# A hybrid decoder block on one Trainium2 core: memory attention one head ahead, x turned once, differential heads left unscaled, last plain panels loaded sooner

## The chip, the cores and the metric
The kernel runs on one core of one Trainium2 chip. The metric is the device time of one execution in microseconds (us). The kernel before was timed in three runs: median 1875.49, from 1874.84 to 1875.73. A core has five engines with an instruction queue each: PE (matrix products and transposes; PEld is its weight load), DVE (VectorE), ACT (ScalarE), POOL (GpSimd) and SP, which only issues transfers here.

## The reference, cut to what matters
x is 1024 tokens by 1024 float32 channels, mem 256 tokens. All weights are float32.

```python
def _hybrid_mixer(h, w_in, ...):          # h = rmsnorm(x) * g_mix
    qa, ka, va, qb, kb, vb, fl, ga, gb = jnp.split(h @ w_in, IN_OFFSETS, axis=-1)
    ...
        a1 = softmax(causal(qa1 @ ka1 * scale + rel)); a2 = softmax(causal(qa2 @ ka2 * scale + rel))
        oa = (a1 - lam * a2) @ va          # 4 differential heads, 128 wide
        ob = softmax(causal(qb @ kb * scale + (c_q - c_k))) @ vb   # 8 forgetting heads
    ya = _rmsnorm(oa, g_subln) * (1.0 - lambda_init)
    return (sigmoid(ga) * (ya @ w_diff_out) + sigmoid(gb) * (yb @ w_fox_out)) @ w_o
def _memory_cross_attention(h, mem_n, w_q, w_kv, w_o):   # 4 heads, 256 wide, 256 keys
    return (softmax(q @ k * 1/16) @ v) @ w_o
def reference(x, mem, ...):
    x = x + _hybrid_mixer(_rmsnorm(x, g_mix), ...)
    x = x + _memory_cross_attention(_rmsnorm(x, g_mem_q), _rmsnorm(mem, g_mem_kv), ...)
    x = x + relu(_rmsnorm(x, g_mlp) @ w1) ** 2 @ w2
    return _rmsnorm(x, g_final)
```

## The kernel before, in words
Activations lie transposed, channels on the partitions, in two halves of 512 tokens. Each float32 operand is kept as a high part, rounded by an ACT copy, and a low part, what is left (a subtraction on DVE or POOL). `mm3` (L100 to L102) makes a product of three matmuls: high by high, low by high, high by low. `wload` (L89 to L96) brings a weight panel into one of two `raw` buffers by an SP transfer and splits it: ACT L95 the high part, POOL (or DVE) L96 the low part. The code is written as stages; a scheduler orders each engine's instructions among them by what it models, so the order on an engine isn't that of the code. Every queue runs in order.

- **Front.** For each of 8 blocks of 128 tokens, `norm1_block` loads x, squares and sums it on ACT (L144), makes 1/rms by `rstd_of` (L135 to L140: small DVE instructions and one ACT square root), scales on DVE by 1/rms and a broadcast copy of g_mix (L146), turns the result by 8 PE transposes (L165), and splits it (L168 ACT, L169 DVE) into `hT`. `xT_block` turns x itself by 8 more transposes (L178), copies it (L180) and stores it for the residual. `v_unit(0)` makes the first values from hT (tiles `vps`, 24 matmuls a block). After that `rel_tables` makes the bias rows (stored and read back through DRAM), and `p_unit(0)` the queries and keys of head 0 (tiles `pq`, `pk`, 96 matmuls).
- **Differential heads** (`scores`, `soft_block`, `pv`, units 0 to 3). Scores plus bias are reduced to their minimum (L380), ACT takes exponentials with their sum (L384), a reciprocal gives z (L385). The second branch's z is multiplied by -lambda (L431), the first branch's row by its z (L432), and L433 adds the second times its factor. PE turns the row (L456), L460 and L461 split it, L483 multiplies it with the values. Work of later stages is drawn from a list of `fillers` in between. The output's rms norm comes in `prep_a_stats`.
- **Memory attention.** For n = 0..7 (4 heads, two token halves): `m_q` makes the queries (`qp`, 48 matmuls), `m_a` goes over 4 token blocks: scores (`msc`, 6 matmuls of 256 columns into a PSUM bank of its own), minimum (L859), exponential (L860), reciprocal (L861), scaling (L862), two transposes (`mtp`, L864); then a split (`mat`, L616 and L617), the product with the values (`mop`) and its split (`mo`). `m_o` multiplies with the output weights (`mop2`, 48 matmuls) and adds to x (L885). `norm_T`, `norm_0a` and `norm_0b` run beside `m_o`; `spread` (L634 to L644, tile `sp`) lays a row of 1/rms over all partitions by PE.
- **Up, first part.** `plain_up(i, c)` multiplies one panel of w1 with one token half. The pairs (2,1) and (3,1) come after `up_weights(0)` has issued its loads and 7 weight splits (`Ring.put`, L1065 ACT and L1066 POOL) for the products that follow (`mm_u`, `o_u`, `sc_u`).

```python
        for mt in range(2):
            T.transpose(tps[mt][:, ss], e[:, mt * P : (mt + 1) * P], ident)
...
w_next, steps = up_weights(0)
do_steps(steps, 7)
for i in range(NP - 6, NP - 4):
    plain_up(i, 1)
```

Of the kernel before, what the change touches and what calls it, by code (L numbers as in the profile page):

```python
# [16 lines left out]
P = 128  # L17
# [23 lines left out]
def trunk(ctx: ExitStack, tc: tile.TileContext, a: dict, out: bass.AP):  # L41
# [40 lines left out]
    def wload(parts, name, eng=G):  # L82

        raw = wp.tile([P, WT], F32, tag="raw", name=f"raw_{name}", bufs=2)
        hl = wp.tile([P, 2 * WT], F32R, tag="hl", name=f"hl_{name}", bufs=3)
        o, views = 0, []
        off = (0, 1024)
        for src, r0, nk, c0, n in parts:
            SP.dma_start(  # L89
                raw[:, o : o + nk * n].rearrange("p (k c) -> p k c", k=nk),  # L90
                src[r0 : r0 + nk * P, c0 : c0 + n].rearrange("(k p) c -> p k c", p=P),
            )
            views.append(tuple(hl[:, x + o : x + o + nk * n].rearrange("p (k c) -> p k c", k=nk) for x in off))
            o += nk * n
        A.copy(hl[:, :o], raw[:, :o])  # L95
        eng.tensor_sub(hl[:, 1024 : 1024 + o], raw[:, :o], f32(hl[:, :o]))  # L96
        return views
# [50 lines left out]
    gmix = att.tile([P, D], F32, tag="bias", name="gmix", bufs=2)  # L148
    xf = a["x"].rearrange("b s d -> (b s) d")

    def norm1_block(sb):
        c, o = sb // 4, (sb % 4) * P
        xb = att.tile([P, D], F32, tag="e1", name=f"xb{sb}", bufs=4)
        SP.dma_start(xb, xf[sb * P : (sb + 1) * P, :])
        if sb == 0:
            SP.dma_start(ident, a["ident"])
            SP.dma_start(gmix, a["g_mix"].partition_broadcast(P))
        xn = att.tile([P, D], F32, tag="kd", name=f"xn{sb}", bufs=4)
        ss = att.tile([P, 4], F32, tag="st", name=f"ss{sb}", bufs=16)
        norm_rows(xb, xn, ss, gmix)  # L160
        for g in range(2):
            ps = bank("tp", f"n1p{sb}_{g}")
            for j in range(4):
                k = 4 * g + j
                T.transpose(ps[:, j * P : (j + 1) * P], xn[:, k * P : (k + 1) * P], ident)  # L165
            p3 = ps.rearrange("p (k s) -> p k s", k=4)
            hi, lo = (hT[c].t[i][g][:, :, o : o + P] for i in (0, 1))
            A.copy(hi, p3)  # L168
            V.tensor_sub(lo, p3, f32(hi))  # L169
        return xb  # L170

    def xT_block(sb, xb):
        c, o = sb // 4, (sb % 4) * P
        for g in range(2):
            ps = bank("o", f"xtp{sb}_{g}")
# [16 lines left out]
    def v_unit(u):  # L192
# [59 lines left out]
    def p_unit(i):  # L252
# [3 lines left out]
        w = {}  # L256
# [75 lines left out]
    def forget_prep():  # L332
# [14 lines left out]
        V.scalar_tensor_tensor(l, z, 0.0, l, ALU.min, ALU.subtract)  # L347
        lt = att.tile([8, S], F32, tag="AT", name="lt", bufs=AT_BUFS)
# [19 lines left out]
    def soft_block(i, x, qb, e, bias_of, tag):  # L368
# [1033 lines left out]
```

## Time and profile before
| | |
|---|---|
| median of three runs | 1875.49 us |
| the profiled execution's own time | 1877.76 us |
| its span | 1875.9 us |
| mean granted clock of PE | 0.988 of full speed |
| busy: PE / PEld / DVE / ACT / POOL | 1805.5 / 1505.1 / 1167.1 / 878.8 / 591.3 us |
| share of the span | 96% / 80% / 62% / 47% / 32% |
| DMA | 207.38 MB, mean 111 GB/s |

The page gives one execution: for each engine its busy time, the span in 40 slices, the chain of work that ended last, and groups of instructions by line and shape with what they waited for. The own time is what the host's timer gives for that execution; the span runs from its first to its last instruction. PE's matmuls overlap in the records, so a matmul's duration there is longer than its step to the next one. [...]

### The profile page before, as it was taken

What the parts mean: (1) busy time and instruction counts of PE and PEld (TensorE: products, weight loads), DVE (VectorE), ACT (ScalarE), POOL (GpSimd) and SP (SyncE); (2) the same over time, 40 slices, a digit from 0 to 9 for tenths busy, and PEclk for the clock granted to TensorE, in tenths of its full rate; (3) what the DMA queues carried; (4) which work ended last, traced back from release to release, by engine and by line L of the source; (5) the groups of instructions that cost most, each with busy time, mean ns of one, the idle gap of its engine ahead of it and who ended that gap; (6) DMA issues with size and microseconds to landing.
All of it is one profiled execution on the core that took longest, in us unless ns stands there. A gap on an engine that the chain in (4) does not pass through costs nothing. (4 is left out here: it accounts for less than half of the span.)

```text
span 1875.9 us, 24763 instructions
## 1 busy us (share of the span) xinstructions
PE 1805.5 (96%) x9110; PEld 1505.1 (80%) x9110; DVE 1167.1 (62%) x2209; ACT 878.8 (47%) x1628; POOL 591.3 (32%) x337
## 2 busy tenths in 40 slices
PE   7999999999999999999999998998999999999998
PEld 7779887787787778888887776787888888887786
DVE  6476877878862442223644658583777775888732
ACT  5455546766775463333443344363333345634421
POOL 2211111111223555433453423205465513132600
PEclk9999999999998999999999999999999999999999
DMA  7411111111224333354332221243444474754311
GB/s 235 140 43 43 46 55 44 54 43 53 56 67 145 105 110 101 90 191 135 112 115 66 79 101 57 88 142 96 141 146 162 136 266 149 238 180 155 123 68 45
DMA packets 234465, 207.38 MB, mean 111 GB/s; under 512 B 12603, under 2 KB 191035, under 8 KB 233832
## 3 DMA queue, kind: packets, MB, share of 16 engines
q1 hardware_dynamic: 219224, 188.76, 32.3%
q10 hardware_dynamic: 15120, 17.04, 2.7%
q8 instruction: 71, 1.16, 0.3%
q14 instruction: 50, 0.41, 0.1%
HBM read 162.73 MB, written 45.40 MB: 111 GB/s over the span
## 5 line engine op out<-in xcount | busy, mean ns | idle before, releaser
L483 PE MATMUL o<-at,v 128*128 128x256 f32 x560 | 106.8, 300 | 3.7 <-ACT at L460 2.1
L483 PEld LDWEIGHTS o<-at,v 128*128 128x128 f32 x560 | 85.2, 193 | 21.7 <-ACT at L460 11.4
L1066 POOL TENSOR_TENSOR hlu<-raw_u,hlu 128x512 fp32r<-128x512 f32 x43 | 67.8, 1590 | 108.0 <-DVE x L967 64.7
L1066 POOL TENSOR_TENSOR hls<-raw_d,hls 128x512 fp32r<-128x512 f32 x32 | 47.2, 1484 | 169.7 <-ACT hls L1065 129.4
L460 ACT CAST at<-tp 128x512 fp32r<-128x512 f32 x120 | 69.1, 585 | 43.1 <-PE tp L456 41.9
L461 DVE TENSOR_TENSOR at<-tp,at 128x512 fp32r<-128x512 f32 x120 | 81.5, 685 | 12.1 <-ACT at L460 11.3
L456 PE MATMUL tp<-ident,e 128*128 128x128 f32 x432 | 77.6, 279 | 9.4 <-DVE at L461 2.5
L1066 POOL TENSOR_TENSOR hls<-raw_u,hls 128x512 fp32r<-128x512 f32 x41 | 63.8, 1565 | 61.3 <-ACT hls L1065 50.3
L456 PEld LDWEIGHTS tp<-ident,e 128*128 128x128 f32 x432 | 52.8, 142 | 25.9 <-DVE tp L458 4.7
L96 POOL TENSOR_TENSOR hl_k<-raw_k,hl_k 128x1024 fp32r<-128x1024 f32 x8 | 19.8, 2480 | 164.8 <-ACT hl_k L95 106.9
L1065 ACT CAST hls<-raw_d 128x512 fp32r<-128x512 f32 x62 | 38.0, 620 | 69.4 <-DVE raw_d L1115 29.9
L96 POOL TENSOR_TENSOR hl_wom<-raw_wom,hl_wom 128x1024 fp32r<-128x1024 f32 x16 | 38.3, 2393 | 93.8 <-ACT hl_wom L95 93.8
L96 POOL TENSOR_TENSOR hl_gb<-raw_gb,hl_gb 128x1024 fp32r<-128x1024 f32 x16 | 38.4, 2398 | 86.6 <-ACT hl_gb L95 47.8
L289 POOL CAST kd<-kd 64x512 fp32r<-64x512 f32 x32 | 20.6, 642 | 117.4 <-ACT kd L287 79.1
L100 PE MATMUL vps<-hl_v,hT 128*128 128x256 f32 x192 | 56.6, 295 | 0.4 <-ACT hT L168 0.2
L102 PE MATMUL vps<-hl_v,hT 128*128 128x256 f32 x192 | 55.3, 288 | 1.3 <-DVE hT L169 1.3
L885 DVE TENSOR_TENSOR x<-x,mop 128x512 f32<-128x512 f32 x64 | 43.6, 683 | 20.7 <-PE mop L102 20.2
L96 POOL TENSOR_TENSOR hl_ga<-raw_ga,hl_ga 128x1024 fp32r<-128x1024 f32 x16 | 38.4, 2398 | 55.6 <-ACT hl_ga L95 43.4
L1065 ACT CAST hlu<-raw_u 128x512 fp32r<-128x512 f32 x43 | 26.3, 620 | 62.1 <-PE mm_u L1036 19.4
L101 PE MATMUL vps<-hl_v,hT 128*128 128x256 f32 x192 | 55.0, 286 | 0.0
L96 POOL TENSOR_TENSOR hl_wo<-raw_wo,hl_wo 128x1024 fp32r<-128x1024 f32 x16 | 38.8, 2427 | 50.8 <-ACT hl_wo L95 47.8
L1065 ACT CAST hls<-raw_u 128x512 fp32r<-128x512 f32 x41 | 25.1, 620 | 61.1 <-PE mm_u L1036 26.3
(813 smaller groups left out, 6436.9 us busy)
## 6 DMA issues: line engine op xcount, KB each, us to landing
raw_u<-in_w_dram SPq DMA_DIRECT2D x48, 256.0 KB, 4.2
sD<-tt SPq DMA_DIRECT2D x12, 1024.0 KB, 5.2
raw_d<-in_w_dram ACTq DMA_DIRECT2D x24, 512.0 KB, 3.4
hs<-sD SPq DMA_DIRECT2D x36, 256.0 KB, 3.9
raw_ga<-in_w_in_dram SPq DMA_DIRECT2D x16, 512.0 KB, 3.8
raw_gb<-in_w_in_dram SPq DMA_DIRECT2D x16, 512.0 KB, 3.9
raw_wo<-in_w_o_dram SPq DMA_DIRECT2D x16, 512.0 KB, 4.0
raw_wq<-in_w_q_mem_dram SPq DMA_DIRECT2D x16, 512.0 KB, 3.7
```

The source lines that it names most:

```text
L96: eng.tensor_sub(hl[:, 1024 : 1024 + o], raw[:, :o], f32(hl[:, :o]))
L100: T.matmul(ps, lh, rh, start=start, stop=False)
L101: T.matmul(ps, lh, rl, start=False, stop=False)
L102: T.matmul(ps, ll, rh, start=False, stop=stop)
L289: G.tensor_copy(t["kd"][x][r2, cs], f32(t["kd"][x][r, cs]))
L456: T.transpose(dst, Aq[qi][:, kb * P : (kb + 1) * P], ident)
L460: A.copy(at[:, 0, :], tp)
L461: V.tensor_sub(at[:, 1, :], tp, f32(at[:, 0, :]))
L483: T.matmul(o[:, :256], vv, aa, start=kp == 0 and n == 0, stop=kp == m and n == len(jobs) - 1)
L885: V.tensor_add(x2(c, j), x2(c, j), ps)
L1065: A.copy(w[0], src)
L1066: eng.tensor_sub(w[1], src, f32(w[0]))
```

## The change
It touches five places.

1. **x turned once.** `x_turn` transposes x itself (tile `xtp`), keeps the copy `xt` (one store a block, `x_store`), and computes 1/rms as before. `norm1_block` spreads 1/rms over the partitions by one transpose (`n1p`), multiplies each of the 8 channel blocks by g_mix (a per-partition column `gx_c`) and by that spread row on DVE (L204), and splits on ACT (L207) and POOL (L208). The loop is skewed: loading, turning, normalising and the first values run one or two blocks apart, and the first query panel's loads, split and part of its matmuls are drawn into the loop.
2. **Differential heads unscaled.** L432 goes; the second branch's factor becomes z2 * -lambda * s1 in one instruction (L460), with s1 the first branch's sum, kept in `dsum`. `prep_a_stats` scales EPS by s1 squared.
3. **`forget_prep`** is drawn in three pieces, with part of the next head's projections between them.
4. **Memory attention.** `m_a` becomes `m_s` (scores and softmax, two token blocks in one bank with one minimum and one reciprocal), `m_t` (transposes and split) and `m_v`; `m_s(n + 1)` is issued between `m_t(n)` and `m_v(n)`. `spread` is parted in two.
5. **Last plain panels.** Panel (2,1) is loaded with (1,1)'s, and (3,1)'s load is written ahead of both products.

```diff
+    def wload2(parts, name, eng=G):
...
+        def split():
...
+        return split
...
-    def norm1_block(sb):
...
+    def x_turn(sb):
...
+        for g in range(2):
+            ps = bank(("tp", "o")[g], f"xtp{sb}_{g}")
             for j in range(4):
                 k = 4 * g + j
                 T.transpose(ps[:, j * P : (j + 1) * P], xb[:, k * P : (k + 1) * P], ident)
...
+        A.activation(tt.rearrange("p k s -> p (k s)"), xb, AF.Square, accum_out=ss[:, 3:4])
+        A.copy(xt[:, 0:4, :], pss[0])
+        (V.tensor_copy if sb % 2 else A.copy)(xt[:, 4:8, :], pss[1])
+        rcol[sb] = (rstd_of(ss, ss[:, 3:4], D, 1), tt)
...
+    def norm1_block(sb):
...
+        ps = bank("sc", f"n1p{sb}")[:, 0:P]
+        T.transpose(ps, r.broadcast_to([P, P]), ident)
+        for g in range(2):
+            for k in range(4 * g, 4 * g + 4):
+                V.scalar_tensor_tensor(tt[:, k, :], xts[sb][:, k, :], gx_c[:, k : k + 1], ps, ALU.mult, ALU.mult)
+            hi, lo = (hT[c].t[i][g][:, :, o : o + P] for i in (0, 1))
+            t = tt[:, 4 * g : 4 * g + 4, :]
+            A.copy(hi, t)
+            G.tensor_sub(lo, t, f32(hi))
...
-                z1 = soft_block(u, 0, qb, e, bf, f"{u}a{qb}")
+                s1 = soft_block(u, 0, qb, e, bf, f"{u}a{qb}", dsum[:, qb // 4, u, qb % 4 : qb % 4 + 1])
                 fill()
                 z2 = soft_block(u, 1, qb, e2, bf, f"{u}b{qb}")
-                V.tensor_scalar(z2, z2, nlam, None, ALU.mult)
-                V.tensor_scalar(e[:, :L], e[:, :L], z1, None, ALU.mult)
+                V.scalar_tensor_tensor(z2, z2, nlam, s1, ALU.mult, ALU.mult)
                 V.scalar_tensor_tensor(e[:, :L], e2[:, :L], z2, e[:, :L], ALU.mult, ALU.add)
...
+    for sb in range(10):
+        if sb < 8:
+            x_turn(sb)
...
+        if 1 <= sb < 9:
+            norm1_block(sb - 1)
+            x_store(sb - 1)
+        if sb >= 2:
+            for _ in va0(sb - 2):
+                if sb >= 6:
+                    next(pu0[0], None)
...
-    def m_a(n):
...
+    def m_s(n):
...
+            st = small(f"mst{n}{pr}")
+            e = me[n, pr] = t2k(f"me{n}{pr}").rearrange("p (b m) -> p b m", b=2)
+            V.tensor_reduce(st[:, 0:2], ps, axis=AX.X, op=ALU.min)
...
+            V.reciprocal(st[:, 4:6], st[:, 2:4])
+            for b in range(2):
+                V.tensor_scalar(e[:, b, :], e[:, b, :], st[:, 4 + b : 5 + b], None, ALU.mult)
+
+    def m_t(n):
...
     for n in range(8):
-        m_a(n)
+        m_t(n)
+        if n < 7:
+            m_s(n + 1)
+        m_v(n)
...
-    for i in range(NP - 6, NP - 4):
-        plain_up(i, 1)
+    w31 = panel(3, 1)
+    plain_up(2, 1, w=wn)
+    plain_up(3, 1, w=w31)
```

DVE's queue in the front, where block 2 is normalised. In a name the first digits are the token block: ss2 holds its sum and 1/rms, xn2 the scaled block, vps0 the first values of block 0. Before:

```order
L146 SCALAR_TENSOR_TENSOR xn1_186<-xb1_184,ss1_187,gmix_96 128x1024
L135 TENSOR_SCALAR ss2_242<-ss2_242 128x1
L137 RECIPROCAL ss2_242<-ss2_242 128x1
L138 TENSOR_TENSOR ss2_242<-ss2_242 128x1
L139 SCALAR_TENSOR_TENSOR ss2_242<-ss2_242 128x1
L140 SCALAR_TENSOR_TENSOR ss2_242<-ss2_242 128x1
L237 TENSOR_TENSOR v0_153<-vps0_0_155,v0_153 128x128
L146 SCALAR_TENSOR_TENSOR xn2_241<-xb2_239,ss2_242,gmix_96 128x1024
L237 TENSOR_TENSOR v1_154<-vps0_0_155,v1_154 128x128
L169 TENSOR_TENSOR hT0_2_87<-n1p1_0_196,hT0_0_85 128x4x128
L169 TENSOR_TENSOR hT0_3_88<-n1p1_1_203,hT0_1_86 128x4x128
```

Now:

```order
L204 SCALAR_TENSOR_TENSOR xn2_197<-xt2_196,gx_c_77,n1p2_297 128x128 x3
L261 TENSOR_TENSOR v0_240<-vps0_0_242,v0_240 128x128
L156 RECIPROCAL ss3_273<-ss3_273 128x1
L204 SCALAR_TENSOR_TENSOR xn2_197<-xt2_196,gx_c_77,n1p2_297 128x128
L189 COPY xt3_271<-xtp3_1_279 128x512
L261 TENSOR_TENSOR v1_241<-vps0_0_242,v1_241 128x128
L157 TENSOR_TENSOR ss3_273<-ss3_273 128x1
L204 SCALAR_TENSOR_TENSOR xn2_197<-xt2_196,gx_c_77,n1p2_297 128x128
L158 SCALAR_TENSOR_TENSOR ss3_273<-ss3_273 128x1
L204 SCALAR_TENSOR_TENSOR xn2_197<-xt2_196,gx_c_77,n1p2_297 128x128
L159 SCALAR_TENSOR_TENSOR ss3_273<-ss3_273 128x1
L204 SCALAR_TENSOR_TENSOR xn2_197<-xt2_196,gx_c_77,n1p2_297 128x128 x2
```

The one 1024-wide L146 of a block and the two low-part subtractions L169 are gone from DVE. Eight 128-wide L204 stand there, and the small instructions of block 3's 1/rms (L156 to L159) stand between those of block 2. POOL's queue, which held nothing in the front but the weight panels' subtractions, now holds two L208 for each block among them.

PE's queue in memory attention, head n = 0, around its transposes (mtp00 is head 0, key half 0; me02 is head 0, token block 2, and in the change me01 is token blocks 2 and 3; mop00 is the product with the values). Before:

```order
L100 MATMUL qp20_9270<-h2_0_1_7904,hl_wq20_9266 128x512
L864 MATMUL mtp00_9179<-ident_69,me02_9219 128x128
L864 MATMUL mtp01_9180<-ident_69,me02_9219 128x128
L101 MATMUL qp20_9270<-h2_0_3_7906,hl_wq20_9266 128x512
L102 MATMUL qp20_9270<-h2_0_1_7904,hl_wq20_9266 128x512
L864 MATMUL mtp00_9179<-ident_69,me03_9234 128x128
L864 MATMUL mtp01_9180<-ident_69,me03_9234 128x128
L100 MATMUL qp20_9270<-h2_0_1_7904,hl_wq20_9266 128x512
L101 MATMUL qp20_9270<-h2_0_3_7906,hl_wq20_9266 128x512
L102 MATMUL qp20_9270<-h2_0_1_7904,hl_wq20_9266 128x512
L100 MATMUL mop00_9246<-mat0_9178,vm0_7909 128x512
L100 MATMUL mop01_9255<-mat0_9178,vm0_7909 128x512
```

Now:

```order
L116 MATMUL msc10_9150<-km_0_7822,qm1_9028 128x256
L933 MATMUL mtp00_9136<-ident_69,me01_9128 128x128
L933 MATMUL mtp01_9143<-ident_69,me01_9128 128x128
L933 MATMUL mtp00_9136<-ident_69,me01_9128 128x128
L933 MATMUL mtp01_9143<-ident_69,me01_9128 128x128
L117 MATMUL msc10_9150<-km_1_7823,qm1_9028 128x256
...
L116 MATMUL msc11_9171<-km_0_7822,qm1_9028 128x256
L117 MATMUL msc11_9171<-km_1_7823,qm1_9028 128x256
L118 MATMUL msc11_9171<-km_0_7822,qm1_9028 128x256
L116 MATMUL mop00_9193<-mat0_9135,vm0_7824 128x512
L117 MATMUL mop00_9193<-mat0_9135,vm0_7824 128x512
```

Before, two transposes stand behind each block's softmax, and the last of them a few query matmuls ahead of mop00. Now the transposes stand together among the scores of head 1, and 17 of the 24 score matmuls of head 1 lie between the last transpose and mop00.

SP's queue at the last plain panels (w1p21 is panel 2 for token half 1; u00 and u01 are the first two loads of the products that follow). Before:

```order
L89 DMA raw_w1p11_11463<-in_w1_dram 128x8x128
L1091 DMA raw_u00_11530<-in_w1_dram 128x4x128 x2
L1091 DMA raw_u01_11533<-in_w1_dram 128x4x128 x2
L89 DMA raw_w1p21_11555<-in_w1_dram 128x8x128
L89 DMA raw_w1p31_11589<-in_w1_dram 128x8x128
```

Now:

```order
L92 DMA raw_w1p11_11298<-in_w1_dram 128x8x128
L92 DMA raw_w1p21_11332<-in_w1_dram 128x8x128
L1167 DMA raw_u00_11370<-in_w1_dram 128x4x128 x2
L1167 DMA raw_u01_11373<-in_w1_dram 128x4x128 x2
L92 DMA raw_w1p31_11394<-in_w1_dram 128x8x128
```

The load of w1p21 now stands ahead of u00 and u01; that of w1p31 stays behind them.

## Rows read from the trace of the kernel before

**Rows 1.** Stretches: start:end, length, PE, PEld, DVE, ACT, POOL busy (count), clock, DMA share, GB/s.
```profile
0.00:57.00 57.00, 46.70 (x327) 41.34 (x328) 36.31 (x100) 32.85 (x72) 11.83 (x12) 1.00 0.72 211
79.00:330.00 251.00, 240.61 (x1447) 208.34 (x1446) 192.74 (x539) 135.89 (x292) 44.86 (x32) 0.99 0.16 45
1000.00:1205.00 205.00, 189.09 (x910) 152.83 (x909) 130.36 (x224) 81.83 (x156) 68.01 (x30) 0.98 0.25 79
1275.00:1300.00 25.00, 20.11 (x76) 15.71 (x75) 7.52 (x8) 7.41 (x12) 11.55 (x8) 0.86 0.39 116
```

**Rows 2.** What PE waited for, whole span: us in total, times, longest.
```profile
PE up L100 <- ACT hl_w1p L95: 4.9, 2, 3.9
...
PE msc L100 <- ACT me L860: 4.4, 3, 2.4
...
PE mtp L864 <- DVE me L862: 4.1, 3, 1.7
...
PE mtp L864 <- DVE mst L861: 3.6, 3, 1.2
...
PE sp L644 <- ACT dg L642: 1.9, 1, 1.9
```

**Rows 3.** Three stretches at a lower granted clock, columns as in rows 1.
```profile
102.20:105.60 3.40, 3.40 (x12) 2.88 (x11) 3.34 (x9) 1.38 (x3) 0.00 (x0) 0.50 0.41 136
1105.70:1109.10 3.40, 2.73 (x12) 2.58 (x13) 1.96 (x9) 1.36 (x5) 0.00 (x0) 0.51 0.58 159
1286.70:1293.50 6.80, 5.81 (x14) 4.46 (x14) 1.40 (x2) 2.37 (x4) 3.01 (x2) 0.50 0.54 156
```

**Rows 4.** Timeline at 98 us: start, duration, engine, line, operands, idle before.
```profile
97.85 0.82 PE L456 MATMUL tp<-ident,e 128*128 128x128 f32 x6
...
98.30 2.37 POOL L96 TENSOR_TENSOR hl_k<-raw_k,hl_k 128x1024 fp32r<-128x1024 f32 x1 [14.73 <-ACT hl_k L95]
...
98.36 2.99 DVE L433 SCALAR_TENSOR_TENSOR e<-e,mn0b,e 128x640 f32<-128x640 f32 x1
...
101.60 0.33 PE L456 MATMUL tp<-ident,e 128*128 128x128 f32 x1 [2.01 <-DVE mn0a L385]
```

**Rows 5.** DVE groups of the front: busy us, mean ns, idle before.
```profile
L169 DVE TENSOR_TENSOR hT<-n1p,hT 128x512 fp32r<-128x512 f32 x16 | 10.6, 683 | 3.1 <-ACT hT L168 3.1
...
L146 DVE SCALAR_TENSOR_TENSOR xn<-xb,ss,gmix 128x1024 f32<-128x1024 f32 x8 | 10.2, 1280 | 1.4 <-DMA gmix<-in_g_mix_dram 1.0 <-DVE ss L137 0.3
...
L237 DVE TENSOR_TENSOR v<-vps,v 128x128 fp32r<-128x128 f32 x14 | 4.0, 286 | 5.1 <-ACT v L236 5.0
```

**Rows 6.** L138's instructions: ns min/median/max, first and last start.
```profile
L138 DVE TENSOR_TENSOR ss<-ss x8: 146/156/728, 6.0 to 34.3; 128x1 f32<-128x1 f32 x8
```

**Rows 7.** The first values' matmuls, columns as in rows 6.
```profile
L100 PE MATMUL vps<-hl_v,hT x64: 277/283/579, 11.2 to 56.0; 128*128 128x256 f32 x64
```

**Rows 8.** POOL low parts: group of the page (busy, mean ns), and one in the timeline.
```profile
L1066 POOL TENSOR_TENSOR hlu<-raw_u,hlu 128x512 fp32r<-128x512 f32 x43 | 67.8, 1590 | 108.0 <-DVE x L967 64.7
...
1265.83 3.44 POOL L1066 TENSOR_TENSOR hlu<-raw_u,hlu 128x512 fp32r<-128x512 f32 x1 [64.72 <-DVE x L967]
```

**Rows 9.** L432 alone between 79 and 330 us: DVE busy (count).
```profile
79.00:330.00 251.00, 17.66 (x32) 0.99 0.16 45
```

**Rows 10.** L862's instructions, columns as in rows 6.
```profile
L862 DVE TENSOR_SCALAR me<-me,mst x32: 337/353/1723, 982.8 to 1204.2; 128x256 f32<-128x256 f32 x32
```

**Rows 11.** Timeline of DVE ahead of tile sp.
```profile
1125.52 2.23 DVE L139 SCALAR_TENSOR_TENSOR trn<-trn 128x4 f32<-128x4 f32 x1
```

**Rows 12.** Timeline of PE at the last plain panels.
```profile
1278.21 0.39 PE L1035 MATMUL o_u<-T,hlu 128*128 128x512 f32 x1
...
1281.38 0.39 PE L1037 MATMUL sc_u<-h,hlu 128*128 128x512 f32 x1
...
1285.67 0.50 PE L100 MATMUL up<-h,hl_w1p 128*128 128x512 f32 x1 [3.90 <-ACT hl_w1p L95]
```

**Rows 13.** Timeline of SP there.
```profile
1279.90 1.62 SPq L89 DMA_DIRECT2D raw_w1p<-in_w_dram  x2
```

More of the change, by code (lines that the diff above doesn't have):

```diff
@@ L92, in wload @@
             )
-            views.append(tuple(hl[:, x + o : x + o + nk * n].rearrange("p (k c) -> p k c", k=nk) for x in off))
             o += nk * n
-        A.copy(hl[:, :o], raw[:, :o])
-        eng.tensor_sub(hl[:, 1024 : 1024 + o], raw[:, :o], f32(hl[:, :o]))
-        return views
+        def split():
+            hl = wp.tile([P, 2 * WT], F32R, tag="hl", name=f"hl_{name}", bufs=3)
+            q, views = 0, []
+            for _, _, nk, _, n in parts:
+                views.append(
+                    tuple(hl[:, x + q : x + q + nk * n].rearrange("p (k c) -> p k c", k=nk) for x in (0, 1024))
+                )
+                q += nk * n
+            A.copy(hl[:, :o], raw[:, :o])
+            eng.tensor_sub(hl[:, 1024 : 1024 + o], raw[:, :o], f32(hl[:, :o]))
+            return views
+        return split
+    def wload(parts, name, eng=G):
+        return wload2(parts, name, eng)()
     def mm3(ps, lh, ll, rh, rl, start, stop):
@@ L196, in v_unit @@
         c0 = (VB if fox else VA) + 256 * (u % 2)
-        panels = []
+        panels = [] if panels is None else panels
         def part(sb):
             if sb == 0:
-                for g in range(2):
+                for g in range(2 - len(panels)):
                     if u == 2:
@@ L358, in forget_prep @@
         SP.dma_start(cD, lt)
+        yield
         ps = bank("tp", "cqp")
@@ L512, in trunk @@
     rel_tables()
-    for f in p_unit(0):
+    for f in pu0:
         for _ in f:
@@ L642, in spread, with spread_2 @@
                     A.activation(dg[:, i, o : o + P], ident, AF.Copy, scale=f32(rh[:, i, sb : sb + 1]))
+            dgs.append(dg)
+        return dgs
+    def spread_2(dgs, name):
+        ps = bank("tp", f"sp{name}")
+        for g in range(2):
             for i in range(2):
-                T.matmul(ps[:, g * 256 : (g + 1) * 256], ones_r, dg[:, i, :], start=i == 0, stop=i == 1)
+                T.matmul(ps[:, g * 256 : (g + 1) * 256], ones_r, dgs[g][:, i, :], start=i == 0, stop=i == 1)
         return ps
@@ L867, in m_a, with m_v @@
+    def m_t(n):
+        at = mat[n] = unit(ATU[n % 2], [P, 2, 2, CH], F32R, f"mat{n}")
+        for mt in range(2):
+            tp = bank("tp", f"mtp{n}{mt}")
+            for sb in range(4):
+                T.transpose(tp[:, sb * P : (sb + 1) * P], me[n, sb // 2][:, sb % 2, mt * P : (mt + 1) * P], ident)
+            split_to(at[:, 0, mt, :], at[:, 1, mt, :], tp, V)
+    def m_v(n):
+        h, at = n % 4, mat[n]
         o = om[n] = unit(OU[n % 2], [P, 2, 2, CH], F32R, f"mo{n}")
```

162 lines of the change are left out of this document (82 added, 80 removed).

## The prediction

> **What bounds the kernel now.** I read the page first: PE is busy for 96% of the span, and the chain that ended last runs mostly through PE. So the time is PE's work plus the places where PE stands or runs slowly, and the question for each part of the change is what it takes from either. The table of stretches [rows 1] gives the places. In the front (0 to 57 us) PE is busy 46.7 us, so it stands for 10.3. Under the differential heads (79 to 330) it stands for 251 - 240.6 = 10.4 us, under memory attention (1000 to 1205) for 205 - 189.1 = 15.9, and at the last plain panels (1275 to 1300) for 4.9. The list of PE's waits [rows 2] names who ended them: in memory attention the score matmuls waited 4.4 us for the exponential of an earlier block, the transposes 4.1 for its scaling and 3.6 for its reciprocal, and the spread row's matmul 1.9. Those four make 14.0 of the 15.9. [...]
>
> A PE step of 512 columns takes (1281.38 - 1278.21) / 14 = 0.226 us [rows 12], and one of 256 columns half of that, 0.11. Six transposes in a row take 0.82 us, the last of them an ordinary duration of 0.27 long, so a step is 0.11 [rows 4].
>
> **The change part by part. (a) The front.** PE does 64 transposes for 8 blocks instead of 128, and 8 more for the spread: 56 fewer at 0.11, 6.2 us less work. But PE had idle time here, so the pace is set by the others. The first values' matmuls run from 11.2 to 56.0 us; a block has 24 of them, 2.7 us, so the last block begins at about 53.4 and a block takes (53.4 - 11.2) / 7 = 6.0 us [rows 7]. DVE does for a block now 1.28 (L146), two times 0.68 (L169), one half copy of about 0.68, two evictions of 0.29 and five small ones of about 0.16: 4.7 us [rows 5, 6]. After the change L146 and L169 go, eight L204 of 128 columns with one operand in PSUM come, nearest to L237 at 0.29 (2.3 us), and the copy falls to every second block: about 4.1 us. GpSimd gets two low parts of 128x512 a block. The nearest row means 1.59 us, its longest 3.44 [rows 8]; half of the 2.37 of a 1024-wide one would be 1.2 [rows 4]. I take 1.3, so 2.6 us a block, and 2.4 more for three weight panels.
>
> Now the catch. At 98.30 GpSimd began a subtraction of 2.37 us, DVE's L433 of 640 columns began at 98.36 and took 2.99 us, and PE stood 2.01 us for what came behind it [rows 4]. L138, one element a partition, takes 0.156 us but 0.73 when it meets the low part of a values panel [rows 6]; L139 on four elements once took 2.23 [rows 11]. The subtractions L169 and L237, with an operand in PSUM, are not lengthened [rows 5]. So L157 to L159, whose operands all lie in SBUF, will each now and then wait for a GpSimd instruction, 24 times in the front, with GpSimd busy over half of the time. Half of these waiting half an instruction (0.65) or a long one's rest costs about 1.2 us a block. The block then takes 4.1 + 1.2, and I take 5.5 with PE's and ACT's turns in between. Bounds: 4.1 without any wait, 7.4 with every GpSimd instruction waited out (2.6 and 0.7 for the panels).
>
> The first values start about 1 us later, at 12.3, since x is turned, scaled and split in more steps. The last block begins at 12.3 + 7 * 5.5 = 50.8, 2.6 us sooner than now. One of the four runs of 24 query and key matmuls (5.4 us) moves into the gaps. Together 8.0; I leave 3 for what this uncovers, above all the bias row, whose way through DRAM before the first scores gets no shorter: **-5 us**, from -9 (no waits, the bias then last) to +6 (7.4 a block: 12.3 + 51.8 = 64.1, 10.7 late, less 5.4 for the moved run).
>
> [...]
>
> **(b) Differential heads.** L432 was 17.7 us of DVE in 32 instructions [rows 9], of 192.7 busy [rows 1]; the 32 reciprocals of s1 go as well, 5 us at 0.156 like L138 [rows 6], and L431's successor costs as much as L431 did. DVE's load falls by a tenth. PE's stands are 10.4 us and the stretch at 102 us costs 1.7, so at most -12; at least 0, since a relieved DVE may only wait longer for ACT. One stand of 2.0 us with its slow stretch follows from a meeting with GpSimd [rows 4], which the change does not remove. I take **-5**, a little under half. Cutting `forget_prep` into three pieces lies inside that. The added instruction in `prep_a_stats` is small and far from a wait: 0.
>
> **(c) Memory attention.** The work stays: 192 query, 192 score matmuls and so on. What goes is PE's waiting: head n + 1's scores, 24 steps of 0.11 (2.7 us), stand between the transposes and the values of head n, and the softmax of a head now has all of `mop2` ahead of its transposes, 48 steps or 10.8 us. The waits of transposes and scores, 4.4 + 4.1 + 3.6 = 12.1 us, should nearly all go, and with them the slow stretch at 1105, 1.7. The wait for the spread row, 1.9 with its own slow stretch, has its cause on DVE [rows 11] and stays. The scaling L862 takes 0.35 us and up to 1.72 [rows 10]; that range stays, but now lies under `mop2`. I leave 1 us for new short waits: **-13**. Ends: -19 if all 15.9 and two slow stretches go; -7 if half of the 12.1 stays, since the exponentials now hold their buffers one head longer and the transposes' PSUM tag is shared with `sp`. One minimum for two token blocks, 16 for 32, only helps DVE.
>
> **(d) Last plain panels.** PE ended its last ready work at 1281.4 + 0.2, and stood 4.1 us until (2,1)'s panel was split [rows 12], because its load was issued at 1279.90 behind u00 and u01 [rows 13]. Now (2,1) is loaded early and its 24 matmuls, 5.4 us, follow (1,1) at 1278 to 1284. But (3,1)'s load still stands behind u00 and u01 and needs a raw buffer that one of them frees; these come later by the buffer that w1p21 took, some 3 us by the splits of 1.3 to 1.6 each [rows 8]. Issued at about 1282.9, it is split about 5 us later, as before (1279.9 to 1285.7): PE waits from 1284 to about 1288.5. The stand moves; the products that PE used to do before it (15 matmuls) now come after. **-1**, from +1.5 to -8 (stand 4.9 and slow stretch 3.4 gone).
>
> **Sum:** -5 - 5 - 13 - 1 = -24. The profiled execution took 1877.76 us on its own (span 1875.9), 2.27 above the median of the three runs, 1875.49. So 1853.8 on its basis, and 1851.5 on that of the runs.
>
> **Rivals.** *Every meeting waited out in the front:* 7.4 us a block, (a) is +6 instead of -5: 1862.5. For it that L433 and L139 waited so long [rows 4, 11]; against it that the small instructions are short and the queue reaches them seldom just as GpSimd starts. With (b) and (c) at their low ends it would come out within 0.2% of before. Chance 0.18, of which 0.04 for that. *Softmax buffers hold memory attention up:* (c) is -7: 1857.5. For it the longer hold; against it that 10.8 us of `mop2` lie ahead. 0.15. *DVE was the whole cause in the differential heads:* (b) is -12: 1844.5. For it that DVE is busy 77% there; against it [rows 4]. 0.13. *The last panel is in time:* (d) is -8: 1844.5. Against it the buffer. 0.10. *Slower: GpSimd becomes the bound of the front.* If its low parts, written in strides of 128, take 3.44 us like the longest row instead of 1.3, 16 of them and three panels are 55 + 7 = 62 us from 10.6 on; the last block's end then stands at 73, 2.7 us of values and three runs of 5.4 follow, 92 us against about 78 now (56.2 and 96 steps of 0.226): +14. With the same long meetings (b) gives 0, (c) -7, (d) +1.5: +8.5, 1884. It decides where two low parts outlast a block, at 2.75 us each. Against it the mean of 1.59 [rows 8]. 0.06. That the change doesn't do what it says holds for (d) alone, and is in the forecast.
>
> **How the numbers follow.** The forecast has 0.38: 1851.5. The range 1837 to 1867 takes in all rivals but the slow one and that of 0.2%, with 7 us below the two at 1844.5 for both or a larger (a), and 4.5 above 1862.5. A measurement here tells 0.2%, 3.8 us, from no change: faster 0.90, the same 0.04, slower 0.06.
>
> **What would show it.** In the profile after: first values from 12 to about 53 us at 5.5 a block, with some of L157 to L159 above 0.6 us; the first matmul of head 1's queries at 72 to 75 instead of about 78; no L432 and no wait of `mtp` for `me` over 0.5 us; PE standing under 5 us between the stages of memory attention; one stand of 4 us before (3,1). A block over 6 us in the front, or waits of `mtp` still near 7 us, would make the prediction wrong.

## The result, and the profile after

The changed kernel took 1851.98 us (median of 4 runs, 1847.27 to 1853.42) against 1875.61 for the kernel before in the same sitting. The ratio is 0.9865 with a 95% interval from 0.9847 to 0.9882: faster, by 23.6 us in the medians. The forecast was 1851.5. The profiled execution is the shortest of the four, 1847.27 us with a span of 1845.5, so its stages add up to 30.4 us of span where the medians show 23.6; the text on the slow stretches below says where the rest may lie.

The page's busy times after, and then the table of stretches with the columns of [rows 1]: the front, the differential heads, memory attention from its first score matmul to its last output matmul, and the last plain panels.

```profile
span 1845.5 us, 24598 instructions
PE 1789.1 (97%) x9054; PEld 1496.1 (81%) x9054; DVE 1144.9 (62%) x2151; ACT 876.5 (47%) x1632; POOL 610.5 (33%) x353
```

```profile
0.00:57.00 57.00, 46.56 (x295) 40.10 (x296) 44.02 (x138) 37.09 (x79) 33.52 (x28) 1.00 0.67 202
73.60:320.00 246.40, 240.66 (x1460) 207.39 (x1460) 173.63 (x482) 137.10 (x295) 45.06 (x32) 1.00 0.18 53
962.60:1192.50 229.90, 221.12 (x1090) 185.11 (x1089) 142.21 (x230) 97.19 (x188) 74.78 (x32) 0.99 0.27 86
1245.00:1270.00 25.00, 20.33 (x80) 15.88 (x79) 9.23 (x10) 7.53 (x13) 13.37 (x10) 0.86 0.34 106
```

PE does 16 us less of busy time. Against [rows 1] it stands 5.7 us under the differential heads (10.4 before), 8.8 in the 230 us of memory attention (15.9 before), and still 4.7 at the last panels. In the front it stands 10.4 us, as much as before. The list of PE's waits after, to be read against [rows 2]:

```profile
PE mop L116 <- DVE x L956: 2.7, 2, 1.8
...
PE mop L117 <- DVE mat L663: 2.6, 2, 1.9
...
PE sp L699 <- ACT dg L691: 1.9, 1, 1.9
...
PE mtp L933 <- DVE h L822: 1.4, 1, 1.4
```

No wait of a transpose or a score matmul for the softmax is left. The product and output matmuls (`mop`) now wait 5.3 us for DVE, the spread row waits 1.9 as before, and the panel 4.6 (shown further below).

Where the stages begin and end on PE, from the groups of single tiles (ns min/median/max, then the first and last start). First the kernel before:

```profile
L377 PE MATMUL s0a<-kd,qs x12: 278/363/628, 79.3 to 110.7; 128*128 128x512 f32 x5, 128*128 128x256 f32 x4, 128*128 128x384 f32 x3
L377 PE MATMUL s4a<-kd,qs x12: 280/338/476, 303.9 to 331.2; 128*128 128x512 f32 x5, 128*128 128x256 f32 x4, 128*128 128x384 f32 x3
L100 PE MATMUL msc<-km,qm x64: 276/283/562, 979.0 to 1202.3; 128*128 128x256 f32 x64
L102 PE MATMUL mop<-mo,hl_wom x128: 389/389/628, 997.4 to 1221.8; 128*128 128x512 f32 x128
L1035 PE MATMUL o_d<-hu1T,hls x28: 389/389/416, 1617.9 to 1685.9; 128*128 128x512 f32 x28
```

Then the changed kernel:

```profile
L404 PE MATMUL s0a<-kd,qs x12: 277/364/473, 73.9 to 101.8; 128*128 128x512 f32 x5, 128*128 128x256 f32 x4, 128*128 128x384 f32 x3
L404 PE MATMUL s4a<-kd,qs x12: 277/338/481, 294.4 to 319.2; 128*128 128x512 f32 x5, 128*128 128x256 f32 x4, 128*128 128x384 f32 x3
L116 PE MATMUL msc<-km,qm x64: 277/283/368, 962.6 to 1152.7; 128*128 128x256 f32 x64
L118 PE MATMUL mop<-mo,hl_wom x128: 388/389/400, 983.3 to 1192.3; 128*128 128x512 f32 x128
L1111 PE MATMUL o_d<-hu1T,hls x28: 389/389/499, 1586.8 to 1655.0; 128*128 128x512 f32 x28
```

The first scores come 5.4 us sooner (79.3 to 73.9), the first forgetting head 9.5 sooner, so 4.1 were won between. Memory attention takes 1192.3 - 962.6 = 229.7 us instead of 1221.8 - 979.0 = 242.8, 13.1 less. A product of the down part (`o_d`) is 31.1 sooner and the last of memory attention 29.5, so the panels gave 1.6. These four make 24.2 us. In that one execution 6.9 more lie between 304 and 979 us (now 294 and 963), where the change does next to nothing, and 0.7 are lost behind `o_d`.

In the front, the groups of the small instructions of 1/rms (L157 to L159), the scaling L204 and GpSimd's low parts L208, ns min/median/max:

```profile
L157 DVE TENSOR_TENSOR ss<-ss x8: 142/156/1266, 6.0 to 39.1; 128x1 f32<-128x1 f32 x8
L158 DVE SCALAR_TENSOR_TENSOR ss<-ss x8: 152/520/2209, 6.2 to 40.4; 128x1 f32<-128x1 f32 x8
L159 DVE SCALAR_TENSOR_TENSOR ss<-ss x8: 143/156/2359, 6.4 to 40.6; 128x1 f32<-128x1 f32 x8
L204 DVE SCALAR_TENSOR_TENSOR xn<-xt,gx_c,n1p x64: 320/338/349, 7.2 to 51.6; 128x128 f32<-128x128 f32 x64
L208 POOL TENSOR_TENSOR hT<-xn,hT x16: 1271/1288/1298, 12.3 to 52.8; 128x512 fp32r<-128x512 f32 x16
```

L208 takes the 1.3 us that was assumed, L204 0.34 instead of 0.29. Each of the three small lines, 0.156 us by itself, reaches 1.3 to 2.4 us where it meets GpSimd. The first values run from 13.7 to 55.4 us, a block from the next by 5.4. At the last panels, PE and the load of panel (3,1):

```profile
1253.79 0.39 PE L118 MATMUL up<-h,hl_w1p 128*128 128x512 f32 x1
1258.81 0.79 PE L116 MATMUL up<-h,hl_w1p 128*128 128x512 f32 x1 [4.63 <-ACT hl_w1p L106]
```

```profile
1253.09 0.37 SPq L92 DMA_DIRECT2D raw_w1p<-in_w_dram  x1
```

PE ends panel (2,1) at 1254 and stands until 1258.8, since the load was issued at 1253.09, behind u00 and u01, and had waited 10.2 us for a raw buffer, by SP's waits until DVE's L1193 was done with it (see also run 7). It is the stand of [rows 12], moved by one panel, and the mean granted clock of the stretch is low again (0.86, as in [rows 1]).

### The profile page after: what moved, and what is told of

It is laid out like the page before. It is cut to its first block, busy times and chain, and to the rows that moved or that the text cites. A ratio compares the mean times of both kernels' runs of the same rounds, so it can differ in the third digit from the quotient of the medians.

```text
span 1845.5 us, 24598 instructions
## 1 busy us (share of the span) xinstructions
PE 1789.1 (97%) x9054; PEld 1496.1 (81%) x9054; DVE 1144.9 (62%) x2151; ACT 876.5 (47%) x1632; POOL 610.5 (33%) x353
## 4 chain that ended last, share of the span: by engine, by line
PE 74%; DVE 10%; DMA 5%; ACT 5%; issue 3%; POOL 3%; SPq 0%; ACTq 0%; DVEq 0%; POOLq 0%
PE o L511 3%; PE tp L484 2%; PE mm_u L1112 2%; PE mm_u L1111 2%; PE mm_u L1113 2%; PE qp L118 2%; PE dn L118 2%; PE dn L116 2%; PE mop L117 2%; PE qp L116 2%; PE qp L117 2%; PE dn L117 2%; PE gpb L118 1%; PE gpb L117 1%; PE mop L116 1%
```

## The experiments

Twelve runs follow; all ratios are to the kernel before on the same chip, with 95% intervals. Runs 5 to 8 and runs 9 to 12 were on two chips, so differences between their medians are a little less sure than ratios (the kernel before took 1876.5 and 1877.6 us there). The first four put one part of the change alone into the kernel before.

**1. The front alone.** The diff's parts on `wload2`, `x_turn`, `norm1_block` and the loop.

> The kernel before with the front alone changed (x turned once, low parts on GpSimd, first query panel drawn in); heads, memory attention and panels as before. Theory (the terms add, each from its own place): first scores at about 74 us instead of 79.3, and 5 us off the time, ratio 0.997. Rival (the later stages only shift, and DVE and the bias row give the gain back under the first heads): first scores earlier, but 0 to 2 us off the time, ratio 0.999 to 1.000.

Measured: 0.9973 (0.9961 to 0.9985), 1870.1 us against 1876.1; first scores at 74.7 us in its profile. The term of 5 us stands, and it comes through to the end.

**2. The heads alone.** L432 out, L431's successor in, `prep_a_stats`, `forget_prep` in pieces.

> The kernel before with the differential heads alone changed (no scaling by the first branch's reciprocal, and forget_prep in three pieces). Theory: 4 to 5 us off, from 79 to 304 us in the profile, ratio 0.9975. Rival (GpSimd's meetings and ACT set PE's stands, not DVE's load): 0 to 1.5 us off, so that the 4 us of the full change there came from its earlier start. Second rival (DVE is the whole cause): 10 to 12 us off.

Measured: 0.9980 (0.9964 to 0.9996), 1870.8 us. In the profile the first scores stand at 79.8 and the first forgetting head at 299.8, 220.0 us apart against 224.6 before. So 4 to 5 us, as forecast. The ratio alone, 0.8 to 6.8 us, would leave room for the first rival; the 4.6 us of the stage fit neither. The edit holds two things, the scaling and `forget_prep`, and this run doesn't part them. The stand of [rows 4] is gone as well, which the forecast had not counted on: with other lengths on DVE that meeting with GpSimd did not happen.

**3. Memory attention alone.**

> The kernel before with memory attention alone changed (scores one head ahead, two token blocks to a bank, spread parted). Theory: 13 us off, all between the first score matmul and the last output matmul, ratio 0.993; the spread row's wait of 1.9 us stays. Rival (buffers held longer): 6 to 8 us off.

Measured: 0.9938 (0.9919 to 0.9957), 1861.7 us. The stage's first and last matmuls in its profile:

```profile
L100 PE MATMUL msc<-km,qm x64: 278/283/365, 971.0 to 1159.6; 128*128 128x256 f32 x64
L102 PE MATMUL mop<-mo,hl_wom x128: 388/389/403, 991.7 to 1199.2; 128*128 128x512 f32 x128
```

It takes 228.2 us instead of 242.8. The rival's 6 to 8 us is outside.

**4. The last panels alone.**

> The kernel before with the last plain panels alone changed. Theory: the stand of PE moves behind panel (2,1) and keeps its 4 to 5 us and its slow stretch; 0 to 1.5 us off, ratio 0.9995. Rival (the early panel hides the wait): 5 to 8 us off, ratio 0.996.

Measured: 0.9996 (0.9984 to 1.0008), no difference. PE waits 5.7 us for the split of panel (3,1) in its profile, against 4.9 for both panels before: the stand has moved. The four parts add up to a ratio of 0.9887; the next run compares.

**5. The change again.** No edit.

> The changed kernel once more, in the same call as the three that edit it. Theory: the four parts measured alone (ratios 0.9973, 0.9980, 0.9938, 0.9996) add up to 0.9887, 21 us; 0.987 to 0.989. Rival (the parts help each other, as by an earlier start of a stage): 0.985 or below.

Measured: 0.9860 (0.9840 to 0.9881), 1849.7 us. The sum 0.9887 lies 0.6 thousandths outside that interval and its own uncertainty is larger (each part 0.001 to 0.002), so a gain of the parts beyond their sum, of 0 to 5 us, can't be told from none.

**6. No meeting with GpSimd in the front.** An operand that is one value per partition takes the place of the second tensor:

```diff
-        V.tensor_mul(t, y, y)
-        V.scalar_tensor_tensor(t, t, -0.5, v, ALU.mult, ALU.mult)
-        V.scalar_tensor_tensor(y, t, 1.5, y, ALU.add, ALU.mult)
+        if w == 1:
+            V.tensor_scalar(t, y, y, None, ALU.mult)
+            V.tensor_scalar(t, t, -0.5, v, ALU.mult, ALU.mult)
+            V.tensor_scalar(y, t, 1.5, y, ALU.add, ALU.mult)
...
```

> The changed kernel with the three last small instructions of a one-column 1/rms written with one SBUF tensor and a per-partition operand each, so that none has two SBUF tensors. Theory (those three meet GpSimd, and the bias row caps what the front gives): none of them over 0.3 us where they took up to 2.36; the block period falls from 5.4 to about 4.7 us and the last first-values matmul ends 4 to 6 us sooner, but the first scores' bias still lands at 75 to 76 us, so only 0 to 2 us off the changed kernel. Rival (no cap): 4 to 6 us off. Second rival (the operands' kind is not what makes them wait): times as before the edit.

The run's label says port; what in the hardware makes an instruction wait, no run shows.

Measured: 0.9860 (0.9840 to 0.9881), 1848.2 us, no difference from run 5. The same three instructions, and the front's two parts, 0 to 20 and 20 to 57 us, in the columns of [rows 1]:

```profile
L158 DVE TENSOR_SCALAR ss<-ss x8: 202/206/214, 6.1 to 37.5; 128x1 f32<-128x1 f32 x8
L159 DVE TENSOR_SCALAR ss<-ss x8: 201/206/215, 6.4 to 37.7; 128x1 f32<-128x1 f32 x8
L160 DVE TENSOR_SCALAR ss<-ss x8: 201/206/215, 6.6 to 38.0; 128x1 f32<-128x1 f32 x8
```

```profile
0.00:20.00 20.00, 12.86 (x56) 11.24 (x57) 8.19 (x35) 13.67 (x26) 13.17 (x14) 1.00 0.93 310
20.00:57.00 37.00, 35.48 (x248) 30.88 (x247) 27.26 (x105) 23.29 (x53) 21.58 (x16) 1.00 0.55 143
```

And the changed kernel's two parts:

```profile
0.00:20.00 20.00, 11.64 (x55) 10.22 (x56) 12.68 (x35) 13.78 (x26) 12.32 (x13) 1.00 0.96 319
20.00:57.00 37.00, 34.91 (x242) 29.88 (x241) 31.34 (x103) 23.32 (x53) 21.20 (x16) 1.00 0.52 138
```

No instruction takes over 0.22 us now, and DVE's busy time from 20 to 57 us falls by 4.1 us. Yet the last first-values matmul comes only 1.3 us sooner (54.1 against 55.4), and first scores at 72.6. A block still follows the one before by 5.5 us. So the theory's time came out, but not its reason: it had that matmul 4 to 6 us sooner and the bias row in the way. DVE's meetings were real, and they cost about 1 us. The table points to why: from 20 us on PE is busy 34.9 of 37 us, and 8.4 of the 10.4 us that it stands lie before 20 us.

**7. The first loads of `up_weights(0)` in the other staging buffers.**

```diff
-    n_raw = [0]
+    n_raw = [2]
```

> The changed kernel with the first two loads of up_weights(0) in the other pair of staging buffers, so that the load of panel (3,1) waits for none of them. Theory (the buffer is what keeps the stand before (3,1)): the stand of 4.6 us and its slow stretch of 6.8 us at half clock go, 7 to 8 us off the changed kernel. Rival (the panel's own split or the weights' splits are late next): a stand of 2 to 4 us before the products, 2 to 4 us off.

Measured: 0.9821 (0.9797 to 0.9844), 1843.7 us, 6.0 off run 5. The stretch of the panels in its profile:

```profile
1237.00:1262.00 25.00, 24.95 (x111) 20.32 (x110) 13.55 (x14) 11.07 (x20) 16.72 (x10) 1.00 0.49 152
```

PE doesn't stand, and the clock is 1.00. The stand before (3,1) was the raw buffer's, as the prediction's part (d) worked out. From the last output matmul of memory attention to the last one of panel (3,1) it is 67.3 us instead of 74.6 in run 5, 7.3 less, the theory's size. About 3 of them are lost again in this profile: at 1503 us PE stands for 2.2, and 3.4 us at a granted clock of 0.50 follow, which run 5's profile doesn't have.

**8. The bias tables sooner.** As run 6, and `rel_tables()` called ahead of block 4 in the loop.

> [...] Theory (the bias row was the cap): the first exponentials' input starts 5 to 8 us sooner than in the changed kernel, and 4 to 6 us are off it. Rival (DVE's work in the front is the cap, and the tables' copies only add to it): 0 to 2 us off.

Measured: 0.9874 (0.9856 to 0.9892), 1852.2 us: if anything slower than run 5. The first scores come at 77.1 us, 3.2 later than in the changed kernel, with block 4's first values at 39.0 instead of 33.6: the tables' work, now ahead of block 4, holds it up. So this run can't say what the bias row would cost by itself; it shows that fetching it sooner this way doesn't pay. In the changed kernel no wait of PE between 57 us and the first scores is for the bias.

**9. The transposes twice.** After run 6 I formed a new theory, that PE's own work paces the front.

```diff
-                T.transpose(ps[:, j * P : (j + 1) * P], xb[:, k * P : (k + 1) * P], ident)
+                for _ in range(2):
+                    T.transpose(ps[:, j * P : (j + 1) * P], xb[:, k * P : (k + 1) * P], ident)
```

> The changed kernel with each of the 64 transposes of x done twice into the same place: 64 more PE steps of 0.11 us, nothing else added. New theory (in the front PE's own work sets the pace, and the gain of the front was the transposes taken off PE; DVE's meetings with GpSimd lie under PE's work): first scores 5 to 7 us later than the changed kernel's 73.8, so about as late as before the change, and 4 to 7 us more time. Rival (the prediction's: DVE and GpSimd set the block's pace, PE has room): 0 to 2 us later.

Measured: first scores and first forgetting head in its profile:

```profile
L405 PE MATMUL s0a<-kd,qs x12: 277/338/479, 80.2 to 107.3; 128*128 128x512 f32 x5, 128*128 128x256 f32 x4, 128*128 128x384 f32 x3
L405 PE MATMUL s4a<-kd,qs x12: 278/338/479, 300.7 to 325.4; 128*128 128x512 f32 x5, 128*128 128x256 f32 x4, 128*128 128x384 f32 x3
```

They are 6.3 us later than in the changed kernel, for 64 steps of 0.11 us = 7.0, and later than in the kernel before. That is the new theory's number and far from the rival's 0 to 2. The time does not bear it out: 1853.5 us in the median is 3.8 over run 5, but the ratio is 0.9862 (0.9847 to 0.9878), like the change's, and 4 to 7 us more would be 0.988 to 0.990. In the profiles the delay stays, against the changed kernel's first one: 6.3 us at the first forgetting head too (300.7 against 294.4) and 6.7 at the first score of memory attention (969.3 against 962.6). How much of it reaches the end is not settled by this run; run 1 says that the front's gain does.

**10. Two blocks to a bank, without the lead.** From run 3:

```diff
-    m_s(0)
...
-        m_t(n)
-        if n < 7:
-            m_s(n + 1)
-        m_v(n)
+        m_s(n)
+        m_t(n)
+        m_v(n)
```

> The kernel before with two token blocks to a bank, one minimum and one reciprocal for both, and the transposes behind the whole softmax, but not one head ahead (scores, softmax, transposes and product of the same head in a row). Theory (the head's lead is what pays): the waits of transposes stay or grow, as all eight now stand behind the last softmax with only query matmuls to fill; 0 to 4 us off the kernel before, or slower, ratio 0.998 to 1.003. Rival (fewer, wider DVE instructions pay): 8 us or more off, ratio 0.996 or below.

Measured: 0.9927 (0.9914 to 0.9940), 1864.4 us: the rival. The stage's ends and the waits of PE in it:

```profile
L100 PE MATMUL msc<-km,qm x64: 277/283/283, 971.9 to 1183.0; 128*128 128x256 f32 x64
L102 PE MATMUL mop<-mo,hl_wom x128: 389/389/398, 990.1 to 1203.5; 128*128 128x512 f32 x128
```

```profile
PE mtp L885 <- DVE me L878: 6.9, 3, 2.6
PE sp L653 <- ACT dg L645: 1.9, 1, 1.9
```

The stage takes 231.6 us, 11.2 less than before. The wait of scores for an exponential (4.4 us in [rows 2]) is gone without any lead, and the waits of transposes, 7.7 in two lines, are 6.9 in one. By its profile the lead adds 3.4; by the ratios, 0.9938 with it and 0.9927 without, it adds nothing that can be told from noise. The scores' tag has two banks. With one block to a bank a third block needs the bank of the first, and in the kernel before all three of those waits, 2.4, 0.8 and 1.2 us, stand at the third block of a head; with two blocks to a bank a head's four fit. That explains the 4.4 us. The edit also halves the minima and reciprocals, puts a head's transposes together and parts `spread`, and this run doesn't say which of these gave the rest.

**11. The spread row's small instructions in PSUM.** Only for the row of memory attention's side work (`n30`):

```diff
+        if name == "n30":
...
+            y, v, yp, t = st[:, 0:4], st[:, 4:8], ps[:, 64:68], ps[:, 68:72]
...
+            V.reciprocal(y, yp)
+            V.reciprocal(yp, yp)
+            V.tensor_mul(t, yp, y)
+            V.scalar_tensor_tensor(t, t, -0.5, v, ALU.mult, ALU.mult)
+            V.scalar_tensor_tensor(yp, t, 1.5, y, ALU.add, ALU.mult)
```

> The changed kernel with the small instructions ahead of the spread row of memory attention reading and writing PSUM, one more of them, so that none has two SBUF tensors. Theory: the one of 2.2 us falls under 0.3, PE's wait for the spread row (1.9 us) goes, with the slow stretch behind it; 2 to 3.5 us off the changed kernel. Rival (ACT's diagonal rows or the order set that wait): 0 to 1 us.

Measured: 0.9823 (0.9810 to 0.9836), 1843.4 us. The instruction that took 2.23 us [rows 11]:

```profile
L682 DVE SCALAR_TENSOR_TENSOR tsn<-tsn,trn x1: 171/171/171, 1102.4 to 1102.4; 128x4 f32<-128x4 f32 x1
```

It ran while a subtraction of GpSimd, 2.40 us from 1102.11 on, was under way. PE no longer waits for the spread row, and the stage takes 226.4 us, 3.3 less than in the changed kernel and 2.9 less than in run 5 (229.3). That is the forecast's number. No slow stretch lies in memory attention, but none does in run 5's profile either, so that isn't the edit's. The time fell by 6.4 us against run 5, twice the stage's gain, and the two intervals just fail to meet. Between those two profiles the stage already begins 5.2 us sooner (960.2 against 965.4), where nothing was edited, so the edit's own worth is put at the 3 us of the stage.

**12. Runs 6, 7 and 11 together.**

> [...] Theory (from the run with own staging, 6 us, and the other two, 1 and 2 to 3): 9 to 10 us off the changed kernel, ratio to before 0.980 to 0.982. Rival (the gains before the panels are lost again at the panels' loads): no better than own staging alone.

Measured: 0.9797 (0.9785 to 0.9810), 1839.8 us (1837.15 to 1841.69): 9.9 us off run 5 and 37.8 off the kernel before; the forecast was 9 to 10 and 0.980 to 0.982. This is the fastest version here, ahead of both kernels.

## Why the prediction was right, point by point, and where it was not

**Size and sum.** The forecast was -5, -5, -13 and -1. Alone, the parts gave ratios worth 5.1, 3.8, 11.6 and 0.8 us (each times 1876); by the landmarks of one profile 5.4, 4.1, 13.1 and 1.6. So every size came out. The reason given came out in (d); in (a) it was wrong, in (b) and (c) wrong for most of the gain. That the sum held as closely as it did is in part luck. The 1.7 and 3.4 us that parts (b) to (d) put on the stretches of [rows 3] are half of their lengths, an estimate, and no run shows the term. What the traces show there is PE's step: of 512 columns 0.427 us in the median at a granted clock of 0.50 and 0.227 elsewhere in the kernel before, and 0.43 against 0.23 at 1261 and 1250 us in the changed one. By that a stretch of 3.4 us costs about 1.6 and one of 6.8 about 3.2, an estimate as well.

**(a) The front.** The failed step is "PE had idle time here, so the pace is set by the others", and with it that DVE's meetings, 1.2 us a block, set the time. The 10.3 us of idle time were read from one row for 0 to 57 us. Cut at 20 us, in the kernel before:

```profile
0.00:20.00 20.00, 11.99 (x64) 10.90 (x65) 10.30 (x26) 11.13 (x22) 8.72 (x10) 1.00 0.82 270
20.00:57.00 37.00, 34.72 (x266) 30.45 (x265) 26.01 (x76) 21.72 (x51) 3.11 (x2) 1.00 0.66 179
```

8.0 of the 10.3 us lie ahead of 20 us, where PE waits 5.1 us for the first transfers and 2.9 for the first block's norm (L146). From there on PE is busy 34.7 of 37 us. That share alone doesn't prove that PE was the pace, since records of matmuls overlap: 266 of them at the 0.12 us from start to start that the last section shows would fill 32 of the 37 us, an estimate. The stretch up to the first scores says more, the kernel before and then the changed one:

```profile
0.00:79.31 79.31, 69.01 (x425) 59.78 (x426) 41.06 (x108) 38.72 (x81) 19.46 (x16) 1.00 0.72 215
0.00:73.86 73.86, 63.42 (x369) 54.01 (x370) 47.47 (x144) 40.91 (x85) 39.72 (x32) 1.00 0.72 207
```

PE has 369 instructions there instead of 425, the 56 fewer that the prediction counted, and is busy for 5.6 us less. It stands for 10.4 us as it stood for 10.3. So the gain is PE's work alone, and nothing of it is standing. Run 6 takes the meetings away and the first scores come 1.2 us sooner than in run 5 (72.6 against 73.8), with no difference in time; run 9 gives the transposes back and they come 6.3 later.

The forecast's 5.5 us a block was right (5.4) from a sum with the wrong terms. The first values began 2.5 us later than before (13.7 against 11.2) and not 1, and the last block 1.6 sooner (51.8 against 53.4) and not 2.6; the 3 us that were left for the bias row, for which PE didn't wait there, took this up. That is luck. The meetings themselves were forecast rightly: nine of the 24 small instructions took over 0.4 us, 10.9 us beyond their usual 0.156 in all, or 1.4 a block. Most of that lay under PE's work. The main place where it did not is the start, behind two of the nine (2.2 and 1.0 us):

```profile
13.61 0.48 PE L201 MATMUL n1p<-ident,ss 128*128 128x128 f32 x1 [1.69 <-DVE ss L159]
```

The traces show this much of the meetings. In the changed kernel's front nine of the 24 small instructions were under way beside a GpSimd instruction; they took 0.45 to 2.36 us, and each ended 13 to 19 ns after that instruction did. The other 15 met none and took 0.14 to 0.16. In run 6, written with one SBUF tensor, 19 of the 24 ran beside GpSimd and none took over 0.22 us; in run 11, with PSUM, the one that had taken 2.23 took 0.17. One SBUF tensor alone isn't enough: in the kernel before five of the 32 L862 [rows 10], of 256 columns, met a subtraction of GpSimd, took 0.52 to 1.72 us instead of 0.35, and ended 0.15 after it. What sets those apart from run 6's is not shown, and a meeting by itself doesn't say whether its wait lies on the path.

**(b) The heads.** Right in size (run 2). The failed step is the stand of [rows 4], "which the change does not remove". From the first scores to the first forgetting head, the kernel before and then run 2:

```profile
79.30:303.90 224.60, 216.27 (x1313) 187.88 (x1312) 172.54 (x486) 118.64 (x259) 41.21 (x29) 0.99 0.16 47
79.80:299.80 220.00, 216.23 (x1318) 187.14 (x1316) 154.14 (x425) 119.69 (x261) 41.77 (x30) 1.00 0.17 48
```

PE's busy time is the same, and its standing falls from 8.3 us to 3.8. 2.0 of that is the stand of [rows 4], which went because the meeting did not come about, and 1.9 is a wait for a tile of `forget_prep`. So the gain comes mostly from two single stands. That a tenth less of DVE's load brought it, as the forecast had it, is not shown.

**(c) Memory attention.** Right in size (run 3). The step that failed first is the cause: the lead of one head was to hide the softmax, and one minimum for two blocks was to be only a help to DVE. Run 10 shows the reverse: with everything but the lead the stage gives 11.2 of its 14.6 us, and the lead 3.4. Of these 3.4, some 1.6, by the steps above, are a stretch of 3.4 us at 0.50 (at 1140 us) that run 10's profile has and run 3's has not; PE stands 8.9 us in the one and 8.7 in the other. The whole stage in the kernel before and in run 10:

```profile
979.00:1221.80 242.80, 226.89 (x1088) 183.67 (x1087) 151.50 (x262) 100.52 (x188) 74.10 (x32) 0.99 0.26 81
971.90:1203.50 231.60, 222.68 (x1088) 183.37 (x1088) 140.54 (x230) 98.68 (x188) 73.90 (x32) 0.99 0.27 85
```

The second failed step is the sum of what goes and stays. The waits of transposes and scores for the softmax did go, all 12.1 us. But I left 1 us for new waits beside the 1.9 of the spread row, and it is 6.7, most of it `mop` waiting for DVE. So the changed kernel stands 8.8 us where the kernel before stood 15.9, 7.1 less and not 11. The other 6 of the 13.1 us are PE's busy time, 221.1 instead of 226.9 for the same number of instructions; some 1.6 of them are one slow stretch fewer, and what made the rest is open. Two errors cancel here. That the spread row's wait stays, and why, was right: run 11 removes the cause on DVE and the wait goes.

**(d) The panels.** Right, with its mechanism: runs 4 and 7.

**Rivals.** The slower one, GpSimd as the bound of the front, needed low parts of over 2.75 us; they took 1.29. The one of meetings waited out was right in that all nine ended with the GpSimd instruction that they met, 13 to 19 ns behind it. It failed because there were nine of them, 10.9 us and not the 3.3 a block that it put in, and because most of that was hidden.

## What to carry to other kernels

Cut a stretch where its limit changes before reading its idle time: an average over the front hid that PE stood in its first third and hardly after. A wait on an engine is worth removing only as far as the engine that paces the stage waits for it: taking the meetings with GpSimd away was worth about 1 us in the front, where they took eleven of DVE's, and 3 us in memory attention, where PE waited for one. And where a PSUM bank is held until its softmax has read it, count the banks first: two blocks to a bank, with half the small instructions, gave 11.2 us of the stage here by the profiles, and running a head ahead 3.4.

## What the runs showed of the hardware that was not expected

**Slow stretches come and go in code that is the same.** From 575 to 700 us, where the gates and mixing run, the mean granted clock (third number from the right) was 0.93 in the kernel before,

```profile
575.00:700.00 125.00, 118.00 (x519) 95.21 (x518) 47.03 (x73) 70.48 (x136) 62.15 (x34) 0.93 0.41 122
```

and in run 3, whose instructions up to memory attention are those of the kernel before in the same order,

```profile
575.00:700.00 125.00, 118.88 (x560) 95.84 (x559) 48.16 (x74) 72.37 (x139) 66.70 (x35) 1.00 0.45 131
```

it was 1.00. In other profiles it was 0.93 (run 9), 0.95 (run 5), 0.97 (the changed kernel and run 11) and 1.00 (run 10). In the kernel before some 17 us of that stretch ran at a granted clock of 0.50, which cost about 8, an estimate from the steps of 0.427 us instead of 0.227: memory attention begins at 979.0 us in the one and at 971.0 in the other. So one profile can stand 8 us from another for a reason outside the change, which is about the size of what was left over in this one and in run 11. In the kernel before the first of these stretches, 10.2 us from 590.3 on, begins behind a stand of PE of 2.05 us for the sums of a norm, and the second, 6.8 us at 651.8, behind none. In run 3 the same stand is 0.83 us and no stretch follows; in run 7 it is 0.51 us, and 10.2 us at 0.50 follow. So the length of that stand doesn't decide it, and what does is open.

**PE's first steps ran at half pace under a clock column of 1.00.** Steps of 256 columns in the kernel before:

```profile
16.39 0.41 PE L100 MATMUL vps<-hl_v,hT 128*128 128x256 f32 x1
...
16.60 0.41 PE L101 MATMUL vps<-hl_v,hT 128*128 128x256 f32 x1
...
17.33 0.28 PE L100 MATMUL vps<-hl_v,hT 128*128 128x256 f32 x1
...
17.45 0.28 PE L101 MATMUL vps<-hl_v,hT 128*128 128x256 f32 x1
```

They are 0.21 us apart up to 16.8 and 0.12 from 17 on, while the column of the clock shows 1.00 throughout. In the changed kernel the pace changes at 17.6 us, in the middle of a run of transposes. It isn't the same in every execution: in run 9's profile the steps are short from 10.3 us on, and long again from 17.4 to 20.4, where the record does show 0.50 (from 17.1, for 3.4 us). In the two kernels' profiles the record doesn't show the slow start; the distance between starts does.
